# A hybrid attention and retention block on one core: the output projection from seven products of quarters

## The chip, the core and the metric

The kernel runs on one core of a Trainium2 chip. A core has TensorE (PE, matrix products), VectorE (DVE, elementwise work), ScalarE (ACT, elementwise functions and casts), GpSimd (POOL) and SyncE (SP, whose queue starts most transfers), each with a queue of its own that it works off in order. The metric is the device time of one execution in microseconds (us), the median of several runs. A profiled execution of the same program gives the trace, whose times count from the start of its span.

## The reference

512 tokens of 1024 channels, in float32. Two branches run side by side on the normalised tokens and are merged by sigmoid gates, one per channel; the merged rows go through the output projection and are added to the input:

```
p_a = jnp.einsum('bsw,wd->bsd', out_a, w_branch_sb[layer])
p_b = jnp.einsum('bsw,wd->bsd', out_b, w_branch_ret[layer])
merged = (jax.nn.sigmoid(m_sb + b_merge[layer, 0]) * p_a
          + jax.nn.sigmoid(m_ret + b_merge[layer, 1]) * p_b)
x = x + jnp.einsum('bsd,de->bse', merged, w_out[layer])
```

`out_a` is stick-breaking attention with 8 heads, gated; `out_b` is chunkwise retention with 4 heads, normalised and gated. All of their inputs are ten projections of the tokens by `w_in` (1024 x 10240).

## The kernel before

Every large product has 512 rows or columns in each operand and runs in `dense` (L211): four PSUM banks of 128x512, eight steps k over the contraction of 1024, and for each bank and step three matmuls (`mm3`, L91). There are three because both operands are kept as a pair of rounded numbers, a high part and a low part (`split`, L114: ScalarE casts the high part, VectorE subtracts it from the source for the low part), and the products high x high, high x low and low x high are added up. A `dense` call so has 4 x 8 x 3 = 96 matmuls of 512 columns. Weights come from `load_split` (L191): SP loads two steps at once (512 KB, two buffers `raw`), ScalarE and VectorE split them into `whi` and `wlo` (two buffers each), and the yield hands them to TensorE. These instructions have high priority: the scheduler, which sets the order of each queue, puts them ahead of others that it could place there. Matmuls and SP's loads keep the order of the program (`keep_in_program_order`).

Attention, retention and the like are generators that `work.step()` (an `Interleaver`, L40) advances between the matmuls of the projections. The order of the projections is the order of the calls from L523 on. The end of the program is: the retention's projections; the two gates `mb0`, `mb1`; `pb0` and `pb1` (two column groups g of `out_b` times its branch weights, banks transposed, so that a bank holds 128 channels of all tokens); behind each the merge (L573 to L577), four times a product with the gate, a sum with `pa[g]` and a split into `mg_hi` and `mg_lo`; then `fin0` and `fin1` (L581), the output projection's two halves of the columns, 192 matmuls together, whose banks hold 128 tokens and 512 output channels. VectorE adds each bank to the residual's tile `xr[g, tb]`, and a transfer stores it. In `fin1` the last two steps run bank by bank (`late`, L217), so that the banks end one after the other.

Of the kernel before, what the change touches and what calls it, by code (L numbers as in the profile page):

```python
# [33 lines left out]
V_BUFS = 14  # L34
# [33 lines left out]
def hybrid_block(ctx, tc, x, x_t, vecs, w_in, w_a, w_b, w_o, cos_t, sin_t, decay, out):  # L68
# [98 lines left out]
    idle = const.tile([P, S], mybir.dt.bfloat16, name="idle")  # L167
# [100 lines left out]
    def token_norm_rows():  # L268
# [5 lines left out]
        for tb in range(NT):  # L274
            rc = tmp.tile([P, P], F32, tag="rc", bufs=2, name="rc")
# [9 lines left out]
    def qk_group(p):  # L285
# [8 lines left out]
        for tb in range(NT):  # L294
            sq = tmp.tile([P, 4, P], F32, tag="sq", bufs=1, name="sqq")
# [34 lines left out]
    def v_group(name, c0):  # L330

        ps = proj(name, ((c0, S),), True)
        got = []
        for sb in range(NT):
            hi = big.tile([P, S], F32R, tag="V", bufs=V_BUFS, name=f"{name}_hi{sb}")
            lo = big.tile([P, S], F32R, tag="V", bufs=V_BUFS, name=f"{name}_lo{sb}")
            r = rx[:, sb : sb + 1]
            nc.scalar.activation(hi, ps[sb], AF.Copy, scale=r)
            nc.vector.scalar_tensor_tensor(lo, ps[sb], r, f32(hi), op0=ALU.mult, op1=ALU.subtract)
            got.append((hi, lo))  # L340
        return got
# [87 lines left out]
    def rope_group(h):  # L429
# [4 lines left out]
        ps[2:] = [big.tile([P, S], F32, tag="O", bufs=16, name=f"rk{h}_{j}") for j in range(2)]  # L434
# [17 lines left out]
    def retention(h, qk, v, gates):  # L452
        hi, lo = qk
        dec = tmp.tile([P, S], F32, tag="dec", bufs=1, name=f"dec{h}")
# [81 lines left out]
    rv[0] = v_group("rv0", C_RV)  # L536
# [113 lines left out]
```

## Time and profile before

| | us |
|---|---|
| median of 3 runs | 664.4 (664.32 to 664.45) |
| the profiled execution | 664.18 |
| its span | 662.4 |
| TensorE busy | 656.3 (99%) |
| VectorE busy | 375.9 (57%) |
| ScalarE busy | 260.7 (39%) |
| GpSimd busy | 50.8 (8%) |

Matmuls are pipelined: one lasts 0.39 us from start to end, and the next starts 0.23 us after it. So the busy share says that TensorE always had one in flight, and the spacing of the starts is what a matmul costs. A group's idle time and its releaser say what an engine waited for; idle time of an engine that nobody waits for costs nothing.

### The profile page before, as it was taken

The numbers are of one execution on the slowest core, as the hardware profiler recorded it, in microseconds if no ns is written. First come the engines' busy times: TensorE is split into PE (matmuls) and PEld (weight loads), VectorE is DVE, ScalarE is ACT, GpSimd is POOL, SyncE is SP. The second block draws the span as 40 slices with busy tenths as digits, with TensorE's granted clock in tenths as the row PEclk, the third lists the DMA queues.
The fourth block names the chain that finished last, engine by engine and source line by source line (L and its number), as shares of the span: only waits on it lengthen the run. The fifth ranks groups of instructions, "written<-read, shape, count | busy, mean of one in ns | idle before, by whom it ended". The sixth has DMA issues, their size and how long they took to land.

```text
span 662.4 us, 7979 instructions
## 1 busy us (share of the span) xinstructions
PE 656.3 (99%) x3096; PEld 546.4 (82%) x3096; DVE 375.9 (57%) x560; ACT 260.7 (39%) x416; POOL 50.8 (8%) x50
## 2 busy tenths in 40 slices
PE   8999999999999999999999999999999999999997
PEld 5888888888888888888888888888888888888886
DVE  6456874587497477632334763844862953544632
ACT  4744534464364554422312342433433443422310
POOL 0051000441000400000000001001001001000000
PEclk9999999999999999999999999999999999999999
DMA  8543223322322323233333323222323322335541
GB/s 288 189 128 96 65 63 96 96 64 65 95 64 64 96 63 96 60 99 96 95 96 111 96 64 106 84 80 81 96 70 106 93 66 64 96 95 161 158 159 63
DMA packets 42182, 65.02 MB, mean 98 GB/s; under 512 B 2848, under 2 KB 19488, under 8 KB 42144
## 3 DMA queue, kind: packets, MB, share of 16 engines
q1 hardware_dynamic: 41568, 63.47, 31.2%
q10 hardware_dynamic: 576, 1.05, 0.4%
q8 instruction: 24, 0.39, 0.3%
q14 instruction: 14, 0.11, 0.1%
HBM read 62.41 MB, written 2.10 MB: 97 GB/s over the span
## 4 chain that ended last, share of the span: by engine, by line
PE 99%; DMA 0%; SPq 0%; ACT 0%; DVE 0%; issue 0%; DVEq 0%; ACTq 0%
PE qk_ps L86 14%; PE rqk_ps L86 13%; PE sg_ps L86 7%; PE v_ps L86 7%; PE ma_ps L86 7%; PE rv_ps L86 7%; PE mb_ps L86 7%; PE rg_ps L86 7%; PE fin_ps L86 7%; PE pb_ps L86 7%; PE pa_ps L86 7%; PE po L86 2%; PE z L86 2%; PE rz L86 2%; PE ro L86 2%; PE pw L89 1%
## 5 line engine op out<-in xcount | busy, mean ns | idle before, releaser
L86 PE MATMUL qk_ps<-qk_hi,xT_hi 128*128 128x512 f32 x128 | 51.5, 411 | 0.9 <-ACT xT_hi L159 0.9
L86 PE MATMUL rqk_ps<-xT_hi,rqk_hi 128*128 128x512 f32 x128 | 50.5, 394 | 0.0
L86 PE MATMUL rqk_ps<-xT_hi,rqk_lo 128*128 128x512 f32 x128 | 50.0, 391 | 0.0
L86 PE MATMUL rqk_ps<-xT_lo,rqk_hi 128*128 128x512 f32 x128 | 50.0, 390 | 0.0
L86 PE MATMUL qk_ps<-qk_lo,xT_hi 128*128 128x512 f32 x128 | 49.8, 398 | 0.0
L86 PE MATMUL qk_ps<-qk_hi,xT_lo 128*128 128x512 f32 x128 | 49.5, 395 | 0.0
L86 PE MATMUL pb_ps<-ob,pb_hi 128*128 128x512 f32 x128 | 39.5, 390 | 0.0
L86 PE MATMUL pa_ps<-oa,pa_hi 128*128 128x512 f32 x128 | 39.4, 389 | 0.0
L116 DVE TENSOR_TENSOR rqk_lo<-rqk_raw,rqk_hi 128x1024 fp32r<-128x1024 f32 x16 | 20.8, 1300 | 23.9 <-ACT rqk_hi L115 23.9
L386 DVE TENSOR_TENSOR_SCAN keep<-keep,zero 128x128 f32<-128x128 f32 (+3 forms) x32 | 27.1, 847 | 7.3 <-ACT keep L384 7.3
L86 PEld LDWEIGHTS qk_ps<-qk_hi,xT_hi 128*128 128x128 f32 x128 | 24.5, 192 | 6.2 <-ACT xT_hi L159 1.8
L86 PEld LDWEIGHTS qk_ps<-qk_hi,xT_lo 128*128 128x128 f32 x128 | 24.5, 191 | 5.4
L189 POOL TENSOR_TENSOR rrr<-ms,m_half 128x4 f32<-128x4 f32 x4 | 4.0, 1007 | 316.3 <-DVE ms L188 316.3
L86 PEld LDWEIGHTS qk_ps<-qk_lo,xT_hi 128*128 128x128 f32 x128 | 24.7, 193 | 4.3
L86 PEld LDWEIGHTS rqk_ps<-xT_hi,rqk_lo 128*128 128x128 f32 x128 | 24.1, 188 | 5.0
L86 PEld LDWEIGHTS pb_ps<-ob,pb_hi 128*128 128x128 f32 x128 | 24.0, 188 | 5.0
L86 PEld LDWEIGHTS pa_ps<-oa,pa_hi 128*128 128x128 f32 x128 | 24.0, 188 | 5.0
L86 PEld LDWEIGHTS rqk_ps<-xT_hi,rqk_hi 128*128 128x128 f32 x128 | 24.1, 188 | 4.7
L86 PEld LDWEIGHTS rqk_ps<-xT_lo,rqk_hi 128*128 128x128 f32 x128 | 24.1, 188 | 4.6
L115 ACT CAST rqk_hi<-rqk_raw 128x1024 fp32r<-128x1024 f32 x16 | 16.8, 1050 | 25.8 <-PE rqk_ps L86 16.5
L116 DVE TENSOR_TENSOR qk_lo<-qk_raw,qk_hi 128x1024 fp32r<-128x1024 f32 x14 | 17.6, 1259 | 15.1 <-ACT qk_hi L115 15.1
L86 PE MATMUL v_ps<-v_hi,xT_hi 128*128 128x512 f32 x64 | 26.1, 408 | 0.0
(185 smaller groups left out, 1709.8 us busy)
## 6 DMA issues: line engine op xcount, KB each, us to landing
rqk_raw<-in_w_in SPq DMA_DIRECT2D x32, 256.0 KB, 3.0
qk_raw<-in_w_in SPq DMA_DIRECT2D x28, 256.0 KB, 3.0
v_raw<-in_w_in SPq DMA_DIRECT2D x8, 512.0 KB, 3.9
sg_raw<-in_w_in SPq DMA_DIRECT2D x8, 512.0 KB, 3.6
rv_raw<-in_w_in SPq DMA_DIRECT2D x8, 512.0 KB, 3.6
ma_raw<-in_w_in SPq DMA_DIRECT2D x8, 512.0 KB, 3.6
pa_raw<-in_w_a SPq DMA_DIRECT2D x8, 512.0 KB, 3.9
rg_raw<-in_w_in SPq DMA_DIRECT2D x8, 512.0 KB, 3.6
```

Of the source, the lines that this page charges most:

```text
L86: tc.keep_in_program_order(nc.tensor.matmul(*a, **k))
L89: tc.keep_in_program_order(nc.tensor.transpose(*a))
L115: nc.scalar.copy(hi, src)
L116: nc.vector.tensor_sub(lo, src, f32(hi))
L189: nc.gpsimd.tensor_tensor(dst, t[:, :width], m_half[:, :width], op=ALU.pow)
L386: nc.vector.tensor_tensor_scan(keep[:, :n][:, ::-1], keep[:, :n][:, ::-1], zero.broadcast_to([P, n]), 1.0, op0=ALU.mult, op1=ALU.add,)
```

## The change

The merged rows and `w_out` are cut into quarters: x11 is the first 256 tokens with the first 512 channels, x12 the same tokens with the other channels, x21 and x22 the other tokens; B11 to B22 are the quarters of `w_out` (512 x 512). The product of two such matrices needs eight products of quarters; here it is put together from seven, of sums of quarters. `strassen` runs them in the order 1, 2, 5, 3, 6, 7, 4:

- product 1 is x11 B11, product 2 is x12 B21, product 5 is s1 (B11 + B12) with s1 = x21 - x22, product 3 is n4 B22 with s2 = s1 - x11 and n4 = x12 + s2, product 6 is s2 (B11 + B12 + B22), product 7 is s3 (B12 + B22) with s3 = x11 - x21, product 4 is x22 (B21 + B11 + B12 + B22). The numbers are those of the code; the fourth in order is product 3, that of n4.
- a product is 2 halves of the contraction x 2 banks x 2 steps x 3 = 24 matmuls of 512 columns.
- the sums of the weights stand in four tiles X, Y, W, Z, in the place of v's: VectorE adds Y and later Z to X, and four transfers that GpSimd starts add to what is in Y and W. Each half of a piece is split into a high and a low part when its product comes near.
- the merged rows are kept in `pa` (whole numbers) and are split into `xT_hi` and `xT_lo`, where the tokens were. VectorE makes s1, s2 and n4 from `pa`, GpSimd makes s3, and each is split too.
- the products 1, 6, 7 and 4 add up in the same two banks `y`; after each product `put` adds its banks to residual tiles or subtracts them, and four of the seven also store.
- `late` now holds for `pb1`.
- the residual's second four loads come earlier, temporary tiles of equal size are shared (`bk` for beta, keep and the decay, `tmp` for the squares), v's rows are in whole tiles, the room for the descriptors of GpSimd's transfers is doubled, and `rv0` first drains the side work until head 3 is done.

```diff
--- before.py
+++ after.py
...
+    def O_tile(name):
+        return big.tile([P, 2, S], F32R, tag="O", bufs=8, name=name)
     def O_pair(name):
-        return [big.tile([P, S], F32R, tag="O", bufs=16, name=f"{name}_{q}") for q in range(2)]
+        t = O_tile(name)
+        return [t[:, q, :] for q in range(2)]
...
+    def V_tile(name, dtype=F32R):
+        return big.tile([P, 4, S], dtype, tag="V", bufs=4, name=name)
+    def bk_tile(name, dtype=F32):
+        return tmp.tile([P, 2, S], dtype, tag="bk", bufs=3, name=name)
...
-            if name == "fin1" and k >= NK - 2:
+            if name == "pb1" and k >= NK - 2:
...
+    def quarter(w, q):
+        return w[q].rearrange("p (k c) -> p k c", k=4)
+    def add_from(dst, src):
+        nc.gpsimd.dma_start(dst, src, accum_op=ALU.add)
+    def halves(t):
+        return t[:, :, :H], t[:, :, H:]
...
+    def made_sums(name, t):
+        hi, lo = (O_tile(f"{name}_{q}").rearrange("p a (b t) -> p (a b) t", b=2) for q in ("hi", "lo"))
+        split(hi, lo, t)
+        sums[name] = (hi, lo)
+    def quarter_sums(name, w, room):
+        n = [0]
+        def pair():
+            n[0] += 1
+            if n[0] % 3 == 1:
+                return bk_tile(f"{name}_bhi{n[0]}", F32R), bk_tile(f"{name}_blo{n[0]}", F32R)
+            return [
+                wpool.tile([P, 2, S], F32R, tag=f"w{q}", name=f"{name}_{q}{n[0]}") for q in ("hi", "lo")
+            ]
+        def part(t, h):
+            return t[:, 2 * h : 2 * h + 2, :]
+        def made(src):
+            hi, lo = pair()
+            split(hi, lo, src)
+            return hi, lo
+        X, Y, W, Z = room
+        with tc.high_priority():
+            for h in range(2):
+                load(part(X, h), part(quarter(w, B11), h))
+                load(part(Y, h), part(quarter(w, B12), h))
+            load(W, quarter(w, B21))
+            load(Z, quarter(w, B22))
+        for h in range(2):
+            with tc.high_priority():
+                got = made(part(X, h))
+                nc.vector.tensor_add(part(X, h), part(X, h), part(Y, h))
+                add_from(part(Y, h), part(quarter(w, B22), h))
+            yield got
+        for h in range(2):
+            with tc.high_priority():
+                got = made(part(W, h))
+            yield got
+        for h in range(2):
+            with tc.high_priority():
+                got = made(part(X, h))
+                nc.vector.tensor_add(part(X, h), part(X, h), part(Z, h))
+                add_from(part(W, h), part(X, h))
+            yield got
+        for t in (Z, X, Y, W):
+            for h in range(2):
+                with tc.high_priority():
+                    got = made(part(t, h))
+                yield got
+    def product(ps, left, pieces, first):
+        for h in range(2):
+            hi, lo = next(pieces)
+            for j in range(2):
+                js = slice(j * P, (j + 1) * P)
+                for i in range(2):
+                    k = 2 * h + i
+                    a, b = (t[:, k, js] for t in left), (hi[:, i, :], lo[:, i, :])
+                    ahi, alo = a
+                    for n, (u, v) in enumerate(((ahi, b[0]), (ahi, b[1]), (alo, b[0]))):
+                        matmul(
+                            ps[j], u, v, start=first and k == n == 0, stop=k == 3 and n == 2,
+                            skip_group_check=True,
+                        )
+                work.step()
+    def strassen(name, w, room, put):
+        def banks(n):
+            return [ps_mm.tile([P, S], F32, tag="mm", name=f"{name}_{n}{j}") for j in range(2)]
+        pieces = quarter_sums(name, w, room)
+        y = banks("y")
+        for n, a in ((1, "x11"), (2, "x12"), (5, "s1"), (3, "n4"), (6, "s2"), (7, "s3"), (4, "x22")):
+            ps = y if n in (1, 6, 7, 4) else banks(f"p{n}")
+            product(ps, tokens(a), pieces, n in (1, 2, 3, 5))
+            put(n, ps)
+    def tokens(a):
+        if a in sums:
+            return sums[a]
+        i, j = int(a[1]) - 1, int(a[2]) - 1
+        return [t[:, 4 * j : 4 * j + 4, i * H : (i + 1) * H] for t in (xT_hi, xT_lo)]
...
-    rv[0] = v_group("rv0", C_RV)
+    rv[0] = v_group("rv0", C_RV, lambda: 3 in oa)
...
     def residual(g):
-        yield 13
+        yield 13 if g == 0 else 1
...
-        hi, lo = T_tile(f"mg_hi{g}"), T_tile(f"mg_lo{g}")
         for j in range(4):
-            t = tmp_tile(f"mg{g}_{j}")
-            nc.vector.tensor_mul(t, ps[j], m[j])
-            nc.vector.tensor_add(t, t, pa[g][:, j, :])
-            split(hi[:, j, :], lo[:, j, :], t)
-        mt.append((hi, lo))
+            t, k = pa[g][:, j, :], 4 * g + j
+            nc.vector.tensor_mul(m[j], ps[j], m[j])
+            nc.vector.tensor_add(t, m[j], t)
+            split(xT_hi[:, k, :], xT_lo[:, k, :], t)
...
-        ps = dense(f"fin{g}", lambda k: tuple(t[:, k % 4, :] for t in mt[k // 4]), w_o, ((S * g, S),), True)
-        queue = nc.scalar if g == 0 else nc.sync
-        for tb in range(NT):
-            n = S // 2 if g == 1 and tb == NT - 1 else S
-            for c in range(0, S, n):
-                cs = slice(c, c + n)
-                nc.vector.tensor_add(xr[g, tb][:, cs], ps[tb][:, cs], xr[g, tb][:, cs])
-                queue.dma_start(out[tb * P : (tb + 1) * P, g * S + c : g * S + c + n], xr[g, tb][:, cs])
+    (x11, x21), (x12, x22) = halves(pa[0]), halves(pa[1])
+    nc.vector.tensor_sub(x22, x21, x22)
+    made_sums("s1", x22)
+    nc.vector.tensor_sub(x22, x22, x11)
+    made_sums("s2", x22)
+    nc.vector.tensor_add(x12, x12, x22)
+    made_sums("n4", x12)
+    nc.gpsimd.tensor_sub(x21, x11, x21)
+    made_sums("s3", x21)
+    def put(n, ps):
+        for j in range(2):
+            last = n == 4 and j == 1
+            g, tb, op = {
+                1: (0, j, ALU.add), 2: (0, j, ALU.add), 5: (1, 2 + j, ALU.add), 3: (1, j, ALU.add),
+                6: (1, j, ALU.subtract), 7: (1, 2 + j, ALU.subtract), 4: (0, 2 + j, ALU.add),
+            }[n]
+            with tc.high_priority():
+                for c in range(0, S, S // 2 if last else S):
+                    cs = slice(c, c + (S // 2 if last else S))
+                    t = xr[g, tb][:, cs]
+                    nc.vector.tensor_tensor(t, t, ps[j][:, cs], op=op)
+                    if n in (2, 6, 7, 4):
+                        queue = nc.scalar if n == 2 else nc.sync
+                        queue.dma_start(out[tb * P : (tb + 1) * P, g * S + cs.start : g * S + cs.stop], t)
+                if n == 5:
+                    t = xr[1, j]
+                    nc.vector.tensor_add(t, t, ps[j])
+    strassen("fin", w_oq, [V_tile(f"fin_w{n}", F32) for n in range(4)], put)
...
```

**Where the order changes.** VectorE's queue, from the second piece of the projection's weights on (in both it is the first row; `pb_ps` are the banks of `pb1`, `mb` its gates, `pa_2836` the second half of the merged rows, `fin_w` the weight tiles). Before:

```order
L116 TENSOR_TENSOR fin_lo_5022<-fin_raw_5019,fin_hi_5021 128x1024
L575 TENSOR_TENSOR mg_0_4995<-pb_ps_4861,mb_0_4703 128x512
L575 TENSOR_TENSOR mg_1_5000<-pb_ps_4862,mb_1_4706 128x512
L576 TENSOR_TENSOR mg_0_4995<-mg_0_4995,pa_2894 128x512
L576 TENSOR_TENSOR mg_1_5000<-mg_1_5000,pa_2894 128x512
L575 TENSOR_TENSOR mg_2_5005<-pb_ps_4863,mb_2_4709 128x512
L116 TENSOR_TENSOR fin_lo_5052<-fin_raw_5049,fin_hi_5051 128x1024
L576 TENSOR_TENSOR mg_2_5005<-mg_2_5005,pa_2894 128x512
L575 TENSOR_TENSOR mg_3_5010<-pb_ps_4864,mb_3_4712 128x512
L576 TENSOR_TENSOR mg_3_5010<-mg_3_5010,pa_2894 128x512
L116 TENSOR_TENSOR mg_lo_4994<-mg_0_4995,mg_hi_4993 128x512
L116 TENSOR_TENSOR mg_lo_4994<-mg_1_5000,mg_hi_4993 128x512
```

After:

```order
L129 TENSOR_TENSOR fin_lo_4982<-fin_w_4943,fin_hi_4981 128x1024
L690 TENSOR_TENSOR mb_0_4631<-pb_ps_4783,mb_0_4631 128x512
L404 TENSOR_TENSOR fin_w_4943<-fin_w_4943,fin_w_4944 128x1024
L691 TENSOR_TENSOR pa_2836<-mb_0_4631,pa_2836 128x512
L690 TENSOR_TENSOR mb_1_4634<-pb_ps_4784,mb_1_4634 128x512
L690 TENSOR_TENSOR mb_2_4637<-pb_ps_4785,mb_2_4637 128x512
L129 TENSOR_TENSOR xT_lo<-pa_2836,xT_hi 128x512
L129 TENSOR_TENSOR fin_lo_5012<-fin_w_4945,fin_hi_5011 128x1024
L691 TENSOR_TENSOR pa_2836<-mb_1_4634,pa_2836 128x512
L129 TENSOR_TENSOR fin_blo_5028<-fin_w_4945,fin_bhi_5027 128x1024
L691 TENSOR_TENSOR pa_2836<-mb_2_4637,pa_2836 128x512
L717 TENSOR_TENSOR xr_0_4973<-xr_0_4973,fin_y_4947 128x512
```

Before, the whole merge of the second half stands in a row with one split between. Now sums and splits of weights stand between its steps, and the merge of the last bank (`pb_ps_4786`) comes after these rows, behind two additions to the residual.

VectorE's queue further on (`s_lo` and `n_lo` are the low parts of s1 to s3 and of n4, `fin_p` the banks of the products 2, 5 and 3). Before, from the end of the merge:

```order
L116 TENSOR_TENSOR mg_lo_4994<-mg_3_5010,mg_hi_4993 128x512
L116 TENSOR_TENSOR fin_lo_5082<-fin_raw_5079,fin_hi_5081 128x1024
L116 TENSOR_TENSOR fin_lo_5112<-fin_raw_5109,fin_hi_5111 128x1024
L116 TENSOR_TENSOR fin_lo_5162<-fin_raw_5159,fin_hi_5161 128x1024
L588 TENSOR_TENSOR xr_0_4973<-fin_ps_5015,xr_0_4973 128x512
L588 TENSOR_TENSOR xr_1_4975<-fin_ps_5016,xr_1_4975 128x512
```

After, from the additions of product 2 on:

```order
L717 TENSOR_TENSOR xr_1_4975<-xr_1_4975,fin_p_5010 128x512
L129 TENSOR_TENSOR fin_blo_5092<-fin_w_4946,fin_bhi_5091 128x1024
L699 TENSOR_TENSOR pa_2836<-pa_2836,pa_2571 128x4x256
L701 TENSOR_TENSOR pa_2836<-pa_2836 128x4x256
L717 TENSOR_TENSOR xr_2_4997<-xr_2_4997,fin_p_5047 128x512
L129 TENSOR_TENSOR fin_lo_5108<-fin_w_4946,fin_hi_5107 128x1024
L717 TENSOR_TENSOR xr_3_4999<-xr_3_4999,fin_p_5048 128x512
L723 TENSOR_TENSOR xr_0_4993<-xr_0_4993,fin_p_5047 128x512
L723 TENSOR_TENSOR xr_1_4995<-xr_1_4995,fin_p_5048 128x512
L129 TENSOR_TENSOR fin_lo_5126<-fin_w_4943,fin_hi_5125 128x1024
L129 TENSOR_TENSOR s_lo<-pa_2836,s_hi 128x1024
L129 TENSOR_TENSOR n_lo<-pa_2836,n_hi 128x1024
```

Before, only splits of weights and the additions of a finished half are left. Now the sums of the rows and their splits stand between additions and splits of weights, and of these splits only that of s3 comes after `n_lo`.

ScalarE's queue around the projection's first matmul (`fin_w_4943` is X, `fin_w_4945` is W, `fin_w_4946` is Z). Before:

```order
L115 CAST pb_hi_4957<-pb_raw_4955 128x1024
L115 CAST fin_hi_5021<-fin_raw_5019 128x1024
L115 CAST fin_hi_5051<-fin_raw_5049 128x1024
L115 CAST mg_hi_4993<-mg_0_4995 128x512
L115 CAST mg_hi_4993<-mg_1_5000 128x512
```

After:

```order
L128 CAST fin_bhi_4955<-fin_w_4943 128x1024
L128 CAST pb_hi_4879<-pb_raw_4877 128x1024
L128 CAST fin_bhi_5027<-fin_w_4945 128x1024
L128 CAST fin_hi_4981<-fin_w_4943 128x1024
L128 CAST xT_hi<-pa_2836 128x512
```

The cast of the first piece of W (B21) now stands ahead of the cast of X's second half and of the merge's casts.

## Rows read from the trace of the kernel before

**Rows 1.** The page: span, part 1 (engine busy), part 4 (the last chain).
```profile
span 662.4 us, 7979 instructions
...
PE 656.3 (99%) x3096; PEld 546.4 (82%) x3096; DVE 375.9 (57%) x560; ACT 260.7 (39%) x416; POOL 50.8 (8%) x50
...
PE 99%; DMA 0%; SPq 0%; ACT 0%; DVE 0%; issue 0%; DVEq 0%; ACTq 0%
```

**Rows 2.** View of waits, TensorE: who was waited for, total, times, longest.
```profile
PE pi L86 <- DVE idle L168: 1.2, 1, 1.2
PE qk_ps L86 <- ACT xT_hi L159: 0.9, 1, 0.9
```

**Rows 3.** Timeline, TensorE: first and last projection matmul (start, duration us).
```profile
614.77 0.39 PE L86 MATMUL fin_ps<-fin_hi,mg_hi 128*128 128x512 f32 x1
...
658.06 0.39 PE L86 MATMUL fin_ps<-fin_hi,mg_lo 128*128 128x512 f32 x1
```

**Rows 4.** View by windows: length, busy time per engine, clock, DMA share, GB/s.
```profile
610.00:640.00 30.00, 30.00 (x134) 24.87 (x133) 17.47 (x22) 7.90 (x10) 0.00 (x0) 1.00 0.49 157
```

**Rows 5.** Timeline, ScalarE, before the projection's first matmul.
```profile
609.30 1.05 ACT L115 CAST fin_hi<-fin_raw 128x1024 fp32r<-128x1024 f32 x1 [4.34 <-PE pb_ps L86]
```

**Rows 6.** Timeline, VectorE, around the projection's first matmul.
```profile
610.38 1.23 DVE L116 TENSOR_TENSOR fin_lo<-fin_raw,fin_hi 128x1024 fp32r<-128x1024 f32 x1 [4.17 <-ACT fin_hi L115]
...
616.02 1.22 DVE L116 TENSOR_TENSOR fin_lo<-fin_raw,fin_hi 128x1024 fp32r<-128x1024 f32 x1
617.15 0.68 DVE L576 TENSOR_TENSOR mg<-mg,pa 128x512 f32<-128x512 f32 x1
617.75 0.68 DVE L575 TENSOR_TENSOR mg<-pb_ps,mb 128x512 f32<-128x512 f32 x1
```

**Rows 7.** Timeline, GpSimd, at 559 us.
```profile
558.98 2.04 POOL L495 TENSOR_TENSOR roraw<-roraw,rrr 128x512 f32<-128x512 f32 x2
```

**Rows 8.** Timeline, VectorE, the same microseconds.
```profile
560.49 1.61 DVE L116 TENSOR_TENSOR mb_lo<-mb_raw,mb_hi 128x1024 fp32r<-128x1024 f32 x1 [2.67 <-ACT mb_hi L115]
```

**Rows 9.** Timeline, VectorE, the last instructions.
```profile
658.48 0.76 DVE L588 TENSOR_TENSOR xr<-fin_ps,xr 128x256 f32<-128x256 f32 x2 [0.67 <-PE fin_ps L86]
```

**Rows 10.** Timeline, SyncE's queue: pb1's last load is the first row's third.
```profile
584.44 11.43 SPq L119 DMA_DIRECT2D pb_raw<-in_w_b  x3
595.92 2.32 SPq L119 DMA_DIRECT2D xr<-in_x  x4
```

**Rows 11.** View by windows: GB/s at the start and when the residual loads.
```profile
2.00:4.00 2.00, 2.00 (x6) 0.76 (x5) 0.42 (x1) 0.22 (x2) 0.00 (x0) 1.00 0.87 272
6.00:8.00 2.00, 2.00 (x6) 1.52 (x6) 1.41 (x3) 0.72 (x1) 0.00 (x0) 1.00 0.81 278
18.00:20.00 2.00, 2.00 (x10) 1.69 (x9) 0.03 (x1) 1.05 (x1) 0.00 (x0) 1.00 1.00 401
...
596.00:598.00 2.00, 2.00 (x11) 1.65 (x10) 1.91 (x5) 0.62 (x1) 0.00 (x0) 1.00 0.57 168
600.00:602.00 2.00, 2.00 (x10) 1.65 (x9) 1.38 (x2) 0.04 (x1) 0.00 (x0) 1.00 0.98 356
```

**Rows 12.** Timeline, TensorE, from the start of the program.
```profile
1.18 3.60 PE L86 MATMUL pi<-idle 128*128 128x512 bf16 x8 [1.18 <-DVE idle L168]
5.65 2.08 PE L86 MATMUL qk_ps<-qk_hi,xT_hi 128*128 128x512 f32 x4 [0.87 <-ACT xT_hi L159]
7.52 1.91 PE L86 MATMUL qk_ps<-qk_lo,xT_hi 128*128 128x512 f32 x4
9.23 1.46 PE L86 MATMUL qk_ps<-qk_hi,xT_lo 128*128 128x512 f32 x4
10.52 1.07 PE L86 MATMUL qk_ps<-qk_hi,xT_hi 128*128 128x512 f32 x4
```

More of the change, by code (lines that the diff above doesn't have):

```diff
@@ L26 @@
 C_MA, C_MB = 8192, 9216
+B11, B12, B21, B22 = range(4)
+H = S // 2
 V_NG, V_BM, V_QG, V_KG, V_RG, V_N = 0, 8, 24, 25, 26, 34
@@ L33 @@
 RAW_BUFS = 2
-V_BUFS = 14
 N_IDLE = 8
@@ L67, in hybrid_block @@
 @with_exitstack
-def hybrid_block(ctx, tc, x, x_t, vecs, w_in, w_a, w_b, w_o, cos_t, sin_t, decay, out):
+def hybrid_block(ctx, tc, x, x_t, vecs, w_in, w_a, w_b, w_oq, cos_t, sin_t, decay, out):
     nc = tc.nc
@@ L165, in hybrid_block @@
     first = first_loads()
-    idle = const.tile([P, S], mybir.dt.bfloat16, name="idle")
+    idle = tmp.tile([P, 2 * S], mybir.dt.bfloat16, tag="tmp", name="idle")[:, :S]
     nc.vector.memset(idle, 0.0)
@@ L259, in token_norm @@
                 s2 = small.tile([P, 2], F32, tag="s2", name="s2")
-                sq = tmp.tile([P, S], F32, tag="sq", bufs=1, name="sqx")
+                sq = tmp_tile("sqx")
                 for c in range(2):
@@ L274, in token_norm_rows @@
         for tb in range(NT):
-            rc = tmp.tile([P, P], F32, tag="rc", bufs=2, name="rc")
+            rc = tmp_tile("rc")[:, :P]
             nc.vector.tensor_copy(rc, rx[:, tb : tb + 1].broadcast_to([P, P]))
@@ L294, in qk_group @@
         for tb in range(NT):
-            sq = tmp.tile([P, 4, P], F32, tag="sq", bufs=1, name="sqq")
+            sq = tmp_tile("sqq").rearrange("p (h d) -> p h d", h=4)
             nc.scalar.activation(sq, raws[tb], AF.Square)
@@ L328, in qk_group, with v_group @@
             work.add(token_norm_rows())
-    def v_group(name, c0):
+    def v_group(name, c0, ready=lambda: True):
         ps = proj(name, ((c0, S),), True)
-        got = []
+        work.drain(ready)
+        hi, lo = V_tile(f"{name}_hi"), V_tile(f"{name}_lo")
         for sb in range(NT):
[L335 to L341, printed above, removed]
+            v_rows(hi, lo, sb, ps[sb])
+        return [(hi[:, sb, :], lo[:, sb, :]) for sb in range(NT)]
@@ L433, in rope_group @@
         hi, lo = T_tile(f"rqk_hi{h}"), T_tile(f"rqk_lo{h}")
-        ps[2:] = [big.tile([P, S], F32, tag="O", bufs=16, name=f"rk{h}_{j}") for j in range(2)]
+        ps[2:] = [tmp.tile([P, S], F32, tag="qraw", bufs=4, name=f"rk{h}_{j}") for j in range(2)]
         for j in range(2):
@@ L453, in retention @@
         hi, lo = qk
-        dec = tmp.tile([P, S], F32, tag="dec", bufs=1, name=f"dec{h}")
+        dec = bk_tile(f"dec{h}")[:, 0, :]
         load(dec, decay[h])
@@ L628, with quarters @@
     )
+    def quarters(w):
+        return np.stack(
+            [
+                w[i : i + S, j : j + S].reshape(4, P, S).transpose(1, 0, 2).reshape(P, 4 * S)
+                for i in (0, S)
+                for j in (0, S)
+            ]
+        )
     cos, sin, dec = _tables()
@@ L636 @@
         "w_b": np.asarray(w_branch_ret).reshape(D, D),
-        "w_o": np.asarray(w_out).reshape(D, D),
+        "w_oq": quarters(np.asarray(w_out).reshape(D, D)),
         "cos": cos,
```

17 lines of the change are left out of this document (10 added, 7 removed).

## The prediction

> **What bounds the kernel now.** I read the page first: TensorE is busy 99% of the span, and the chain of work that ended last is TensorE to 99%, with every other engine at 0% [rows 1]. The view of waits then says whether it ever stops: twice, 2.1 us in all, both in the first six microseconds [rows 2]. So the time is the number of matmuls times their spacing, and a removed matmul is worth its whole spacing as long as its operands still come in time. The stage of the change is the last one. Its first matmul starts at 614.77 us and its last, the 192nd, at 658.06 [rows 3], so the spacing is 43.29 / 191 = 0.2266 us. Call 614.77 T; all times below are counted from T. Ahead of T the change leaves the order of all 2900 matmuls as it is.
>
> The second thing to read is what feeds TensorE there. In the window 610 to 640 VectorE is busy 17.47 of 30 us and ScalarE 7.90 [rows 4]. That is the share that hides today, and it is what the change spends.
>
> **What goes away.** 7 products of 24 matmuls, all with 512 columns, are 168 in place of 192: 24 x 0.2266 = 5.44 us less TensorE work.
>
> **What is added on VectorE, and why it is on the path.** The queue of an engine is worked off in its order, so I count what stands in VectorE's queue ahead of the operands that TensorE wants. The start is anchored: a split of a piece of weights needs a buffer that TensorE frees 24 matmuls before T (T - 5.44), ScalarE casts, VectorE subtracts. Before, this cast is at 609.30 = T - 5.47 [rows 5] and the subtraction at 610.38 = T - 4.39 [rows 6]. The same pair of buffers stands in the same place after the change, so VectorE again starts at T - 4.39.
>
> From that instruction to the low part of the rows of the fourth product in order, that of n4 (n_lo, the last thing that this product waits for), the queue now holds 37 instructions. 17 have 1024 elements a lane: 8 splits of weight pieces, 3 sums of weight quarters, 3 sums of row quarters, 3 splits of such sums. 20 have 512: the merge of the four banks (4 products, 4 sums, 4 splits) and 8 additions of finished products into the residual. Start to start, 1024 elements take 617.15 - 616.02 = 1.13 us and 512 take 617.75 - 617.15 = 0.60 us [rows 6]. The sum is 17 x 1.13 + 20 x 0.60 = 31.2 us.
>
> Three hold-ups come on top. The split of the first sum (s1_lo) waits for ScalarE's cast of it, 1.05 us by the cast of the same size [rows 5], and only one addition (0.60) stands between: 0.5. VectorE reads results that it has only just written in four places; no row shows the price alone, so 0 to 1 us, and I take 0.5. The third is the subtraction on GpSimd for s3. It needs the same sum as s1, so it starts together with that cast; 1024 elements take 2.04 us as two halves [rows 7]. A VectorE subtraction with both inputs in SBUF that started at 560.49, while GpSimd ran until 561.02, took 1.61 us [rows 8], that is 0.53 of standing still and 1.08 of work. s1_lo falls inside GpSimd's 2.04 us and is held about 1.0 (0 if GpSimd is late, 2.0 if it comes just ahead). The Trainium skill says the same of the cause (SBUF — State Buffer, two separate sides): the two engines share a port pair that is an exclusive lock, and a VectorE operation with two SBUF inputs is blocked for the whole of a GpSimd instruction that reads SBUF. By that rule the hold-up is there and the sum is as it stands; with no lock it would be 1.0 less. The trace agrees with the rule, with the 1.61 us above.
>
> So n_lo ends at -4.39 + 31.2 + 0.5 + 0.5 + 1.0, and 0.1 until the result is written: T + 28.9. TensorE without any wait would ask for it at its 75th matmul, T + 74 x 0.2266 = T + 16.8. It waits 12.1 us up to there. Where these microseconds fall does not change the sum: about 3.5 us when the second half of product 2 wants the last merged bank (its multiplication stands behind two weight splits and the additions of product 1), 2 to 3 us for s1, 5 to 6 us for n4.
>
> From n_lo on 94 matmuls are left. VectorE is ahead again, but the running banks of products 1, 6, 7 and 4 are read by an addition before the next of these products adds to them. Between 1 and 6 other products run; 7 follows 6 and 4 follows 7 at once, and there TensorE waits for the addition: 0 to 0.7 each (one addition), I take 0.4, together 0.8. After the last matmul nothing changes: the last bank is still added in two halves [rows 9], and it still ends six matmuls after the one before it.
>
> **What is added on the queues.** SP now issues six loads of weights, 4.19 MB, at once behind pb1's last load, and the residual's eight loads stand behind them. That last load goes out at about 595.5 and the residual's follow at 595.92 [rows 10], so the weights start there. ScalarE's cast of the first piece of B21 stands ahead of the cast that anchors VectorE, and it waits for a 1 MB load that is the fifth in line: 3.67 MB with pb1's load. By an estimate bytes flow from 596.9 on (168 GB/s over 596 to 598), and with the queue full they flow at 272 to 401 GB/s [rows 11]. B21 lands between 606.1 and 610.4; it is wanted at 609.30 - 1.05 = 608.25. So it costs 0 to 2.1 us; at 360 GB/s it is 607.1 and costs nothing. But GpSimd's first adding transfer (0.52 MB) runs in the same time and would take 1.4 us of that rate: 608.5. I take 0.3. The residual's last load waits for the merge of the last bank at some T + 8 and is used at T + 22, which hides it. The other adding transfers (no row shows one) are issued by T + 13 and wanted at T + 34 and T + 39; up to 20 us each is hidden. The two stores on ScalarE's queue wait for product 2's additions, and the casts of s2 and n4 stand behind them; these end some 4 us before n_lo, so VectorE stays last.
>
> **The other edits** (shared temporary tiles, values in whole tiles, the drain ahead of rv0): taken at 0. TensorE's order is the same and it waits nowhere there [rows 2], so they cannot gain; VectorE at 57% and ScalarE at 39% [rows 1] cover them. If a shared tile is held too long, it shows as a wait of the size of the two in [rows 2], so 0 to 1.2 us.
>
> **The sum.** -5.44 + 12.1 + 0.8 + 0.3 = +7.8 us. The profiled execution took 664.18 us, its span 662.4 and 1.8 around it; the median of the runs is 664.4, 0.2 above. 664.18 + 7.8 = 672.0, and 672.2 for a median.
>
> **Rivals.**
> *VectorE is not the bound and the saved matmuls are the whole story.* TensorE's 99% and VectorE's 17.47 of 30 us speak for it. It decides at n_lo: at T + 16.8 or sooner the time is 664.4 - 5.4 = 659.0; up to T + 21.4 (16.8 + 5.44 - 0.8) it is not slower than before. For that VectorE must do the 37 instructions in 19.1 to 23.7 us in place of 31.2 (2.0 us more if nothing holds it up), or start 7.5 us sooner than its buffer allows. No row shows a two-input operation of 512 elements under 0.60.
>
> *The clock falls in the pauses.* At the start, with TensorE fresh from idling and again after a pause of 0.87 us, four matmuls take 7.52 - 5.65 = 1.87 us, 0.47 each, and it is not before 10.52 that four take 0.91, 0.227 each [rows 12], though the granted clock reads 1.00 throughout [rows 11]. 512 columns in 0.42 to 0.47 us is the 1.2 GHz level. The trace of before holds no later pause. After it there are pauses of some 3.5 us and of 2 and 3.4 us nearly end to end. Price: the second half of product 2 (12 matmuls) takes 12 x 0.2 = 2.4 us more, and an addition that VectorE's queue waits for passes on about 2; after the last pause 4 us at half rate, as from 5.65, lose 2, and 8 us, as from 1.18, lose 4. Together +4 to +6: 676 to 678. The Trainium skill (TensorE: Matmul & The Clock Gate, why this matters for your kernels) asks for no long pauses between bursts of matmuls, since the clock then goes back to half; by that rule this rival is the forecast. The trace agrees only in that a start from idle is slow.
>
> *The weights come late.* Adding transfers cost the queue more than their bytes, and B21 lands 4 to 6 us after 608.25; each microsecond moves the whole of VectorE's stretch: 676 to 678. The low rate of 272 GB/s speaks for it, the 401 against it.
>
> **Chances.** Forecast 0.66 (from +4.7, with no hold-up, late wait or late load, to +11.7, with all at their upper ends: 669.1 to 676.1), clock 0.19, weights 0.08, VectorE not the bound 0.05, a mixture that lands within 0.2%, which is about what a measurement can tell from no change, 0.02. The range 668.5 to 678 takes in the first three. Faster by over 0.2% 0.05, within it 0.02, slower 0.93.
>
> **What would show it.** Right: in the profile after, TensorE has 24 matmuls fewer and some 13 us of waits, all after the first projection matmul, on VectorE and ScalarE; VectorE is busy nearly without a gap from T - 4 to T + 29 while TensorE is not; the longest waits are at the last merged bank and at n4; the tail after the last matmul is the old 4.3 us. The lock shows as an s1_lo of about 2 us. Wrong: TensorE keeps its 99%; or the matmuls after the pauses are 0.4 us apart (clock); or ScalarE's cast of B21 ends later than T - 5.5 and waits for its load (weights); or waits turn up ahead of T (the other edits).

## The result, and the profile after

The changed kernel takes 673.3 us, the median of four runs (672.20 to 674.52), against 664.42 for the kernel before in the same job (664.32 to 664.57): a ratio of 1.0143, 95% interval 1.0128 to 1.0158. It is slower, and 673.3 lies 1.1 us above the predicted 672.2 and inside the range.

The page of the profiled execution (672.84 us) answers to [rows 1]: 24 matmuls fewer, VectorE 22.7 us busier, and the chain that ended last is no longer TensorE alone. The PEclk row, in tenths of full speed over 40 slices, has two slices below 9 near its end.

```profile
span 671.1 us, 7980 instructions
...
PE 654.5 (98%) x3072; PEld 542.2 (81%) x3072; DVE 398.6 (59%) x585; ACT 269.3 (40%) x426; POOL 53.6 (8%) x55
...
PEclk9999999999999999999999999999999999999879
...
PE 91%; DVE 5%; DMA 2%; issue 1%; ACT 1%; SPq 0%; DVEq 0%; ACTq 0%
```

The view of waits for TensorE (total us, times, longest) answers to [rows 2]. Everything new lies in the last stage, 10.6 us in all, on VectorE and ScalarE.

```profile
PE fin_p L89 <- ACT xT_hi L128: 3.6, 1, 3.6
PE fin_p L89 <- DVE n_lo L129: 2.9, 1, 2.9
PE fin_p L89 <- ACT n_hi L128: 2.1, 1, 2.1
PE pi L89 <- DVE idle L181: 1.2, 1, 1.2
PE qk_ps L89 <- ACT xT_hi L172: 1.0, 1, 1.0
PE fin_p L89 <- DVE s_lo L129: 1.0, 1, 1.0
PE fin_y L89 <- DVE xr L717: 0.7, 2, 0.4
PE fin_p L89 <- DVE xT_lo L129: 0.4, 1, 0.4
```

The first and the last projection matmul, the timeline of TensorE, answer to [rows 3]. T is now 612.77, and the last matmul starts 54.09 us later, where it was 43.29.

```profile
612.77 0.39 PE L89 MATMUL fin_y<-fin_bhi,xT_hi 128*128 128x512 f32 x1
...
666.86 0.39 PE L89 MATMUL fin_y<-fin_hi,xT_lo 128*128 128x512 f32 x1
```

So the stage is 10.80 us longer, and yet the span only 8.7: T itself is 2.00 us earlier than in [rows 3]. That gain is the start of the program. In [rows 12] three groups of four matmuls are slow; here none is, the groups start 0.9 to 1.0 apart from 5.75 on:

```profile
5.75 1.19 PE L89 MATMUL qk_ps<-qk_hi,xT_hi 128*128 128x512 f32 x4 [0.96 <-ACT xT_hi L172]
6.78 1.08 PE L89 MATMUL qk_ps<-qk_lo,xT_hi 128*128 128x512 f32 x4
7.69 1.07 PE L89 MATMUL qk_ps<-qk_hi,xT_lo 128*128 128x512 f32 x4
```

The view by windows of the last stage (length, busy time with counts for PE, PEld, DVE, ACT, POOL, then granted clock, DMA share, GB/s) shows the rest. The first of these rows is the stretch that the prediction's queue of 37 instructions fills: VectorE is busy 32.86 of its 33.45 us. The other rows are two short stretches behind TensorE's long pauses and one behind its short one.

```profile
608.80:642.25 33.45, 23.53 (x93) 17.76 (x91) 32.86 (x38) 13.52 (x15) 5.01 (x4) 0.91 0.54 132
...
626.40:629.60 3.20, 3.17 (x8) 2.49 (x9) 2.67 (x3) 1.04 (x1) 2.42 (x2) 0.50 1.02 205
632.00:636.00 4.00, 4.00 (x19) 3.29 (x18) 3.96 (x5) 2.00 (x2) 0.00 (x0) 1.00 0.18 66
...
642.30:646.70 4.40, 4.40 (x10) 3.51 (x11) 1.23 (x2) 0.00 (x0) 0.00 (x0) 0.50 0.00 0
```

TensorE's granted clock is 0.50, its 1.2 GHz level, from 626.4 on, behind the pause that ended at 625.34, and behind the two that ended at 638.65 and 642.30; behind the wait of 1.0 us for s1 it is 1.00. The matmuls show it by their spacing, 0.43 us:

```profile
638.65 0.51 PE L89 MATMUL fin_p<-fin_bhi,n_hi 128*128 128x512 f32 x1 [2.14 <-ACT n_hi L128]
...
642.30 0.80 PE L89 MATMUL fin_p<-fin_bhi,n_lo 128*128 128x512 f32 x1 [2.92 <-DVE n_lo L129]
642.89 0.63 PE L89 MATMUL fin_p<-fin_bhi,n_hi 128*128 128x512 f32 x1
643.32 0.63 PE L89 MATMUL fin_p<-fin_blo,n_hi 128*128 128x512 f32 x1
...
646.73 0.40 PE L89 MATMUL fin_p<-fin_hi,n_hi 128*128 128x512 f32 x1
646.96 0.40 PE L89 MATMUL fin_p<-fin_lo,n_hi 128*128 128x512 f32 x1
```

From 642.30 to 646.73 ten matmuls start, in 4.43 us where 10 x 0.2266 = 2.27 would do: 2.2 us lost. The timelines of ScalarE, VectorE and GpSimd show the queue's start and the lock:

```profile
606.77 1.05 ACT L128 CAST fin_bhi<-fin_w 128x1024 fp32r<-128x1024 f32 x1 [3.82 <-DMA fin_w<-in_w_oq]
607.73 1.04 ACT L128 CAST fin_hi<-fin_w 128x1024 fp32r<-128x1024 f32 x1
```

```profile
608.80 1.23 DVE L129 TENSOR_TENSOR fin_lo<-fin_w,fin_hi 128x1024 fp32r<-128x1024 f32 x1 [4.02 <-ACT fin_hi L128]
...
628.75 2.43 DVE L129 TENSOR_TENSOR s_lo<-pa,s_hi 128x1024 fp32r<-128x1024 f32 x1 [0.52 <-ACT s_hi L128]
631.11 0.67 DVE L717 TENSOR_TENSOR xr<-xr,fin_p 128x512 f32<-128x512 f32 x1
...
641.03 1.22 DVE L129 TENSOR_TENSOR n_lo<-pa,n_hi 128x1024 fp32r<-128x1024 f32 x1
```

```profile
627.72 2.37 POOL L703 TENSOR_TENSOR pa<-pa 128x1024 f32<-128x1024 f32 x1 [0.78 <-DVE pa L697]
```

### The profile page after: what moved, and what is told of

Its sections match the earlier page's. It is cut to its first block, busy times and chain, and to the rows that moved or that the text cites. A ratio compares the mean times of both kernels' runs of the same rounds, so it can differ in the third digit from the quotient of the medians.

```text
span 671.1 us, 7980 instructions
## 1 busy us (share of the span) xinstructions
PE 654.5 (98%) x3072; PEld 542.2 (81%) x3072; DVE 398.6 (59%) x585; ACT 269.3 (40%) x426; POOL 53.6 (8%) x55
## 4 chain that ended last, share of the span: by engine, by line
PE 91%; DVE 5%; DMA 2%; issue 1%; ACT 1%; SPq 0%; DVEq 0%; ACTq 0%
PE qk_ps L89 13%; PE rqk_ps L89 13%; PE sg_ps L89 7%; PE v_ps L89 7%; PE ma_ps L89 7%; PE rv_ps L89 7%; PE mb_ps L89 7%; PE rg_ps L89 7%; PE pa_ps L89 6%; PE pb_ps L89 4%; PE po L89 2%; PE z L89 2%; PE rz L89 2%; PE ro L89 2%; PE fin_y L89 2%; DMA fin_w<-in_w_oq 2%
## 5 line engine op out<-in xcount | busy, mean ns | idle before, releaser
L503 DVE TENSOR_TENSOR_SCAN beta<-beta,zero 128x128 f32<-128x128 f32 (+3 forms) x32 | 26.9, 840 | 7.8 <-ACT beta L501 7.8
```

Of the source, the lines that this page charges most:

```text
L503: nc.vector.tensor_tensor_scan(keep[:, :n][:, ::-1], keep[:, :n][:, ::-1], zero.broadcast_to([P, n]), 1.0, op0=ALU.mult, op1=ALU.add,)
```

## The experiments

The times of one kernel vary by 2 us and more, before's too (662.34 to 664.40 in one job), so I compare the stage, from the first projection matmul's start to the last one's, in the profiled execution; the start of the program is not in it. Each stage below is that of a single execution, and stages vary as well: e4's runs lie 3.3 us apart, more than the start explains (T differs by 2.4 us among the ten profiled executions). So a difference of 1 us between two stages counts only where the rows show what it is made of. The extra matmuls of e2 and e5 do not count as waits.

| kernel | stage us | waits in it | median of runs |
|---|---|---|---|
| before | 43.29 | 0 | 664.42 |
| after | 54.09 | 10.6 | 673.3 |
| e1, two halves again | 43.29 | 0 | 662.62 (10 runs) |
| e2, pauses filled | 53.80 | 3.4 | 673.84 (4) |
| e3, s3 on VectorE | 53.09 | 9.2 | 673.52 (4) |
| e4, two products swapped | 47.75 | 5.7 | 668.45 (4) |
| e5, e4 with one pause filled | 48.95 | 4.7 | 669.11 (5) |
| e6, a written order | 39.20 | 0.3 | 658.15 (5) |
| e7, e6 with ten idle matmuls | 39.21 | 0.3 | 658.04 (4) |
| e8, eight additions later | 49.42 | 7.3 | 668.97 (4) |

**e1, the seven products undone.**

```diff
-    strassen("fin", w_oq, [V_tile(f"fin_w{n}", F32) for n in range(4)], put)
+    for g in range(2):
+        ps = dense(f"fin{g}", lambda k: (xT_hi[:, k, :], xT_lo[:, k, :]), w_o, ((S * g, S),), True)
...
```

> The seven products are undone: the last projection is again two halves of 96 matmuls in before's order, while all the other edits stay (merged rows in the tokens' place, shared temporary tiles, values in whole tiles, the drain ahead of rv0). The trace of after reaches its first projection matmul 2.0 us earlier than that of before, because the matmuls of the first stage run 0.227 us apart from 5.75 us on in place of 0.47. Theory A: this comes with the other edits, which otherwise cost and gain nothing: 664.4 - 2.0 = 662.4 us, no wait of TensorE ahead of the last stage, last stage 43.3 us from first to last matmul. Theory B: it comes with the execution and not with the edits: 664.4, and the start is slow or quick as it falls. Theory C: the other edits cost something at the end (rows merged in place): above 664.9, with waits on VectorE or ScalarE in the last stage.

662.62 us (662.02 to 664.22) against 664.03 for before (662.34 to 664.40), ratio 0.9987, interval 0.9976 to 0.9998. The first and the last projection matmul:

```profile
614.33 0.39 PE L89 MATMUL fin_ps<-fin_hi,xT_hi 128*128 128x512 f32 x1
...
657.62 0.39 PE L89 MATMUL fin_ps<-fin_hi,xT_lo 128*128 128x512 f32 x1
```

The stage is the old one to the hundredth and nothing waits ahead of it, so theory C is out: the other edits cost nothing. The start was slow in the profiled execution (T = 614.33), though the edits are all in it, and both kernels' runs cover the same 2 us: theory B, the start falls by the execution. The traces agree: their first clock record begins at 10.02 us in before's execution, 9.58 in e1's and 5.00 in after's, and there the matmuls turn quick. The median 1.4 us lower says at most that it falls quick more often here; why is open. All of the loss belongs to the seven products.

**e2, the pauses filled.** An extra matmul multiplies merged rows that are long ready into a bank that nobody reads.

```diff
+                        if (n0, h, j, i, n) in FILL:
+                            fill(FILL[n0, h, j, i, n])
...
+    FILL = {(2, 1, 0, 1, 0): 15, (5, 0, 0, 0, 2): 4, (3, 0, 0, 0, 0): 9, (3, 0, 0, 0, 2): 12}
```

> After, with 40 extra matmuls of 512 columns that fill most of the four pauses: 15 ahead of the matmul that waited 3.6 us, 4 ahead of the one that waited 1.0, 9 and 12 ahead of those that waited 2.1 and 2.9 (15 x 0.227 = 3.4, 0.9, 2.0, 2.7 us). They multiply rows that are long ready, into a bank that nobody reads. Clock theory: TensorE does not stop, so no stretch of matmuls 0.43 us apart is left; the end comes 2.0 us sooner (the stretch behind n_lo lies on the path, the one behind the last merged bank does not): 672.8 - 2.0 = 670.8, and the runs spread less. Rival: the matmuls behind a pause are slow for another reason (their operands, the weight loads, VectorE's traffic): the 0.43 us spacing stays in the same places, and the time is 672.8 or more, since the fillers are in the way.

The view by windows: behind the filled pause in product 2, behind a pause of 0.5 and 2.0 us that stayed at s1, and behind the filled ones at n4.

```profile
627.40:629.70 2.30, 1.87 (x7) 1.22 (x7) 2.19 (x3) 1.07 (x2) 1.52 (x2) 1.00 1.00 201
633.80:636.50 2.70, 2.70 (x8) 2.13 (x7) 2.67 (x3) 1.05 (x1) 0.00 (x0) 0.50 0.00 0
645.30:648.00 2.70, 2.70 (x13) 2.25 (x12) 0.85 (x2) 0.24 (x1) 0.00 (x0) 1.00 0.00 0
```

Where TensorE did not stop for more than 0.5 us, the clock stays at 1.00 with the same operands; where it still stopped for 2.0, it falls. That is the clock theory, and the rival is out. The 2 us were gained where they were expected, but lost again ahead of that place. The rows are n_lo on VectorE, its first matmul and the last matmul (T = 613.83):

```profile
643.33 1.22 DVE L129 TENSOR_TENSOR n_lo<-pa,n_hi 128x1024 fp32r<-128x1024 f32 x1
```

```profile
645.29 0.39 PE L89 MATMUL fin_p<-fin_bhi,n_lo 128*128 128x512 f32 x1
...
667.63 0.39 PE L89 MATMUL fin_y<-fin_hi,xT_lo 128*128 128x512 f32 x1
```

From that matmul to the last one it takes 22.34 us, where after takes 24.56: 2.2 less. But the matmul itself starts at T + 31.46, where after's starts at T + 29.53. Of these 1.9 us, 1.2 are n_lo's result, which comes at T + 30.72 in place of T + 29.48: the scheduler moved two of VectorE's instructions ahead of s1's low part, the pause at s1 grew, nine matmuls behind it lost 1.7 us at half rate, and VectorE then stood 1.71 us for a cast of weights that waited for TensorE. The other 0.7 are the extra matmuls, still running when n_lo was there. So the stage is 0.3 shorter and not 2.0, the median is 673.84 in place of 670.8, and the runs lie 3.0 us apart (671.14 to 674.12), not closer.

**e3, the lock.**

```diff
-    nc.gpsimd.tensor_sub(x21, x11, x21)
+    with tc.issue_after(done["n4"].ins):
+        nc.vector.tensor_sub(x21, x11, x21)
```

> After, with the subtraction for s3 on VectorE right behind the low part of n4 in place of GpSimd; everything ahead of that keeps its place in VectorE's queue. Theory (lock on the path): the low part of s1 takes 1.22 us in place of 2.43, n_lo ends 1.2 us sooner, TensorE's waits on s1 and n4 shrink by 1.2 in sum, and the time is 671.6. Rival (the hold-up is absorbed, since TensorE waits for ScalarE's casts as well): s1's low part is quicker, but n_lo and the end come within 0.3 us of where they were. The runs of after lie 2.3 us apart, so the profile decides.

VectorE's timeline, s1's low part, the addition of product 2 behind it, and n_lo:

```profile
628.70 1.23 DVE L129 TENSOR_TENSOR s_lo<-pa,s_hi 128x1024 fp32r<-128x1024 f32 x1 [0.51 <-ACT s_hi L128]
629.84 0.68 DVE L718 TENSOR_TENSOR xr<-xr,fin_p 128x512 f32<-128x512 f32 x1
...
639.79 1.22 DVE L129 TENSOR_TENSOR n_lo<-pa,n_hi 128x1024 fp32r<-128x1024 f32 x1
```

1.23 us in place of 2.43, n_lo 1.24 earlier (T is 612.79), the wait for s1 gone from the view of waits, the stage 1.00 shorter (the stretch at half rate is one matmul longer). So the lock was on the path: 1.2 us of VectorE's queue, 1.0 of the stage. The runs (671.86 to 673.87) can't tell it from after's.

**e4, n4 asked for later.**

```diff
-        for t in (Z, X, Y, W):
+        for t in (X, Z, Y, W):
...
-        for n, a in ((1, "x11"), (2, "x12"), (5, "s1"), (3, "n4"), (6, "s2"), (7, "s3"), (4, "x22")):
+        for n, a in ((1, "x11"), (2, "x12"), (5, "s1"), (6, "s2"), (3, "n4"), (7, "s3"), (4, "x22")):
...
-                    if n in (2, 6, 7, 4):
+                    if n in (2, 3, 7, 4):
```

> After, with the product of s2 ahead of that of n4 (order 1, 2, 5, 6, 3, 7, 4; the weight pieces follow their products). n4's rows are then asked for 24 matmuls = 5.44 us later. VectorE's work is the same, except that the split of s2 moves ahead of the weight pieces of the later products. Theory (the time is set by when the products' operands leave VectorE's queue): the waits of 2.1 and 2.9 us for n4 go nearly whole and no new one of their size comes at s2, whose rows are ready by about 22.9 us after the first projection matmul, when TensorE, held up by the last merged bank and by s1 as before (some 8 us), wants them; the stage is some 4.5 us shorter and the slow stretch behind n_lo goes with its pause (2 us): 666.3, between 665.5 and 668.5. Rival (VectorE's total up to the end of its stretch decides, whatever the order): the wait reappears at s2 and at the weight pieces, and the time is 672 to 674.

668.45 us (666.42 to 669.75), ratio to before 1.0071, interval 1.0047 to 1.0095. The stage is 6.34 shorter, where 4.5 + 2 was expected. In the view of waits n4 costs 0.2 in place of 5.0 and s2 costs nothing:

```profile
PE fin_p L89 <- ACT xT_hi L128: 3.0, 1, 3.0
PE fin_p L89 <- DVE s_lo L129: 2.2, 1, 2.2
...
PE fin_p L89 <- DVE n_lo L129: 0.2, 1, 0.2
```

So not VectorE's total decides, but when TensorE asks for what. The scheduler changed one more thing: here the addition of product 2 and a split of weights stand ahead of s1's low part. The addition waits for TensorE, and the wait for s1 is 2.2 in place of 1.0:

```profile
629.57 0.69 DVE L717 TENSOR_TENSOR xr<-xr,fin_p 128x512 f32<-128x512 f32 x1 [1.59 <-PE fin_p L89]
```

**e5, e4 with the pause in product 2 filled.** The edit is e2's, with `FILL = {(2, 1, 0, 1, 0): 12}`.

> The kernel with the two products swapped, and 12 extra matmuls of 512 columns (2.7 us; rows that are long ready, into a bank that nobody reads) ahead of the matmul that waits 3.0 us for the last merged bank. VectorE's and ScalarE's queues stay as they are, in the same order. In the swapped kernel ten matmuls behind that pause are 0.43 us apart or more, and VectorE's addition of product 2 stands 1.59 us for TensorE. Clock theory: TensorE does not stop, the second half of product 2 runs 0.227 apart, VectorE's addition no longer waits, s1's low part and all that follows come 1.6 us sooner: stage (first to last projection matmul) 46.1 in place of 47.75. Rival (the matmuls are slow for another reason, or the slow stretch is absorbed): stage 47.5 to 48.

The stage is 1.2 longer, so the expectation fails, and the rows say how. Product 2's second half now runs at 1.00 and VectorE's addition doesn't wait for TensorE. But VectorE then meets GpSimd's subtraction of 2.38 us: the instruction ahead of s1's low part is held for 1.0, which in e4 fell into the wait for TensorE. s1 comes only 0.34 us sooner, TensorE is there more than 1 us sooner, waits 0.4 and 2.9 us for it, and runs at 0.50 behind that. The first row is VectorE's timeline, the second the view by windows:

```profile
630.54 2.23 DVE L129 TENSOR_TENSOR fin_blo<-fin_w,fin_bhi 128x1024 fp32r<-128x1024 f32 x1
```

```profile
634.30:637.00 2.70, 2.70 (x8) 2.11 (x7) 2.67 (x3) 1.05 (x1) 0.00 (x0) 0.50 0.00 0
```

Again the half rate goes with the pause and not with the operands. But a pause that is filled is not a wait that is gone: what VectorE has not done is asked for all the sooner. The medians, 669.11 and 668.45, are too close to tell this by themselves.

**e8, eight additions behind n4.** (Product 5's two banks come from the pool that is free by then.)

```diff
-            put(n, ps)
+            held.append((n, ps))
+            if n not in (1, 2, 5):
+                with tc.issue_after(done["n4"].ins):
+                    for m in held:
+                        put(*m)
```

> After, in the order of products that after has, with one thing moved: the eight additions of products 1, 2 and 5 into the residual (8 x 0.60 = 4.8 us of VectorE) stand behind the low part of n4 in place of ahead of it, and product 5 goes to two banks that are free by then. Theory (the wait for n4 is VectorE's queue, instruction by instruction): n4's rows are ready 3 to 4.8 us sooner, the stage is 3 to 4 us shorter (50 to 51 in place of 54.1), with a new short wait where a late addition frees a bank. Rival (the pauses only move to another place): 53 us or more.

n_lo on VectorE (T = 613.09), and the longest waits of the stage:

```profile
634.87 1.23 DVE L129 TENSOR_TENSOR n_lo<-pa,n_hi 128x1024 fp32r<-128x1024 f32 x1
```

```profile
PE fin L89 <- ACT s_hi L128: 4.7, 1, 4.7
...
PE fin L89 <- DVE s_lo L129: 1.3, 1, 1.3
```

The stage is 4.67 shorter, more than the 3 to 4 that were expected; but more was moved than the eight additions. The scheduler put two splits of weights behind n_lo as well, so VectorE's queue up to it has 27 instructions in place of 37, and n_lo's result comes at T + 23.01 in place of T + 29.48. The 6.5 us are 8 x 0.60 + 2 x 1.13 = 7.1, less 0.6 because s1's low part waits longer for ScalarE's cast (1.11 in place of 0.52). n4 is not waited for any more; s1's rows are, 4.7 and 1.3 us, a wait that takes in what the last merged bank's was. What the additions alone are worth is not shown.

**e6, the order written out.** The work is that of e3, in e4's order of products, with some weight pieces split in two halves of 512, and with product 5 and one bank of product 3 in the other pool of banks; each instruction of VectorE and ScalarE is pinned behind the one ahead of it in the text. Its core:

```diff
+RING = ("bk", "qraw", "tmp", "w", "w")
...
+    p3 = piece_hi(part(W, 1))
+    piece_lo(p2)
+    low(2)
+    low(3)
+    prod(1, "x11")
+    pin(nc.vector.tensor_sub(x22, x21, x22))
+    p4 = piece_hi(part(X, 0))
+    sum_hi("s1", x22)
+    piece_lo(p3)
+    prod(2, "x12")
+    piece_lo(p4)
+    p5 = piece_hi(part(X, 1))
+    sum_lo("s1", x22)
+    plus(X, Z, 0)
...
```

> The seven products with VectorE's and ScalarE's work of the last stage in a written order: the swapped order of products; merges of the last four banks first, each sum and its split as early as its product needs it; five pairs of buffers for weight pieces in place of three (the two more in tiles that lie idle by then); the additions of finished products 2 and 5 behind everything that a product waits for; the subtraction for s3 on VectorE. The sum of VectorE's work is the same but for GpSimd's subtraction (+1.1 us). Theory (what bounds after is the order in which VectorE reaches the operands, not their number): TensorE waits 0.5 to 2.5 us in all, no pause is long enough for a slow stretch, the stage is 168 x 0.2266 + 1 to 2.5 = 39 to 40.5 us in place of 54.09 and of before's 43.29: 658.0 to 661.0 us, below before. Rival (VectorE's total is too much for 38 us of TensorE in any order): waits of 5 us and more stay, 664 or above.

658.15 us (658.01 to 659.84), ratio to before 0.9913, interval 0.9899 to 0.9927: 5.7 us faster than before in the same job, and 15 us below after's median. Waits of TensorE, and a window from four microseconds ahead of its first projection matmul (614.65) to 32 behind it:

```profile
PE pi L90 <- DVE idle L182: 1.2, 1, 1.2
PE qk_ps L90 <- ACT xT_hi L173: 0.7, 1, 0.7
PE fin_y L90 <- DVE fin_lo L698: 0.3, 1, 0.3
```

```profile
610.68:646.65 35.97, 35.52 (x156) 28.69 (x155) 35.80 (x46) 17.50 (x23) 2.64 (x3) 1.00 0.43 108
```

VectorE is as full as in after, 35.80 of 35.97 us, and TensorE 35.52, at a granted clock of 1.00 throughout. 39.20 us is 167 x 0.2266 = 37.84 and 1.4. Stage and time lie in the ranges that were expected, and the rival is out.

**e7, e6 with ten idle matmuls at the start.** The edit is one number, `N_IDLE = 10` in place of 8.

> The kernel with the written order, and 10 in place of 8 idle matmuls at the start, which reach nearly up to the first matmul of the program (there is a pause of 0.5 to 1.3 us behind the eight). Theory (the 2.0 us by which executions of one kernel differ are the matmuls of the first stage, slow or quick by what TensorE did in that pause): the first matmuls are 0.23 apart in every execution, the runs lie within 0.5 us, at the lower end of the kernel with eight: 1 us or more below its median. Rival: the pause has nothing to do with it, the spread of 2 us stays, and the median is that of the kernel with eight, within 0.4.

658.04 us (657.55 to 658.58), ratio to before 0.9912, interval 0.9898 to 0.9926; not told from e6. The profiled execution started quick, but the ten took no longer than the eight (3.68 us against 3.59), so the pause stayed, 0.64 us. The experiment did not do what it was to do; it settles nothing about the start.

## Why the prediction was right, and where not

- *24 matmuls fewer, VectorE bounds the stage.* Right, and shown from both sides: with the products undone nothing waits (e1), and with nearly the same work reordered the waits go (e4, e6). So the bound is VectorE's queue in the order in which it stood, and not the sum of its work.
- *The queue of 37.* 33.3 us were predicted, from T - 4.39 to n_lo's result at T + 28.9; 33.45 were measured, from 608.80 = T - 3.97 to 642.25 = T + 29.48. The sum was right to a per cent, since each duration came from a row of the same size. Its three hold-ups were taken at 0.5, 0.5 and 1.0 and came to about 0.6, 0.3 and 1.2.
- *The lock.* Predicted 1.0 for s1's low part, measured 2.43 - 1.22 = 1.2, and by e3 on the path. GpSimd's 1024 elements took 2.37 us in one piece, where [rows 7] gave 2.04 for two halves. The Trainium skill's rule (SBUF — State Buffer, two separate sides) agrees with the 2.43, and with 1.23 once GpSimd is out.
- *B21.* Predicted 0.3, measured 0.43: its cast waited for the load until 606.77, so the next one, which anchors VectorE, starts at 607.73 = T - 5.04, where it was T - 5.47 [rows 5].
- *The bank waits.* 0.8 predicted. With the restart of the matmuls behind them they and the rest of the way cost 1.3: from 646.73 to 666.86 83 matmuls should take 18.81 us, and take 20.13.
- *The clock.* This is the step that failed: it was at nothing in the sum and among the rivals with 0.19, and it came. Behind n_lo it cost 2.2 us, near the lower of the two prices there (2). Its other half did not come: the half rate in product 2 was to be passed on by VectorE's addition, but that addition (631.11) waits for nothing, since s1's low part stands ahead of it in VectorE's queue. In e3, without the lock, it waits for nothing either (629.84); in e4, where it stands ahead of s1's low part, it waits 1.59. What product 2 lost at half rate, 1.6 us, TensorE would else have stood for s1: that wait is 1.0 where 2 to 3 were forecast, and the waits together are 10.6 where some 13 were. The Trainium skill's rule (TensorE: Matmul & The Clock Gate, why this matters for your kernels), no long pauses between bursts, agrees with the 0.50 behind the pause of 3.6 us and the two of 2.1 and 2.9; the wait of 1.0 was followed by 1.00. The prediction's reading that the clock is 1.00 at the start [rows 11] is none: the trace of before holds no clock record ahead of 10.02 us, and the view prints 1.00 where it has none.
- *The other edits at 0.* Right (e1).

The stage was forecast at 43.29 + 7.8 = 51.1 us and took 54.09: 0.3 of the 3.0 is n_lo's lateness, 2.2 the clock, 0.5 the bank waits. That the time still came within 1.1 us of the forecast is because the start of the profiled execution was 2.0 us quicker than that of before's. Started like [rows 12], this execution would have taken 674.8. So the direction and the bound were right by their reasons, and that the time came so close is luck: two misses cancel.

What the prediction did not see is that the loss was not in the idea. It counted VectorE's 37 instructions as a sum that has to be done; it did not ask which of them TensorE needs by then. The eight additions need not stand there (e8, with two splits of weights: 4.7 us of the stage), n4 need not be fourth (e4: 6.3), the subtraction on GpSimd need not run beside s1 (e3: 1.0). All of it together, with the merges first and five pairs of buffers for weight pieces, is 14.9 us (e6); what the buffers, the merges or the other banks give alone was not tried.

## What to carry to other kernels

An algebraic trick that trades matmuls for vector work is decided by the order in which the vector engine reaches the operands: list its queue with the moment at which TensorE asks for each result, before judging the sum. Here the kernel gave the additions of finished products high priority, and the scheduler put them ahead of operands; writing the order out, with two more pairs of buffers, took the stage from 54.1 to 39.2 us with nearly the same instructions. And price a pause of TensorE at more than its length, by what the matmuls behind it do, where no later wait takes that in.

## What the runs showed of the hardware

- Behind the pauses of 3.6 us and of 2.1 and 2.9 in a row (after) and of 0.5 and 2.0 (e2) the granted clock read 0.50 for 7, 10 and 9 matmuls, 1.6, 2.2 and 1.7 us lost. It read 0.50 as well behind 0.4 and 2.9 (e5), 3.0 (e4) and 4.7 and 1.3 (e8). Behind 1.0 us (after), and behind 2.2 us right after such a stretch (e4), the matmuls were quick.
- At the start of the program matmuls are 0.47 us apart, in before's execution up to some 10 us [rows 12]. The view by windows prints a clock of 1.00 there [rows 11], but the trace holds no record of the clock ahead of 10.02 us: the spacing tells it.
- That moment differs by execution: the first clock record of the ten profiled ones begins between 3.96 and 10.60 us, between none and twelve of the first matmuls were slow, and T lies between 612.34 and 614.77.
- A VectorE subtraction of 1024 elements with both inputs in SBUF took 2.43 us beside a GpSimd subtraction of 2.37 (after) and 1.23 without it (e3).
- An adding transfer of 0.52 MB held GpSimd for 0.9 to 1.1 us and landed 5.4 us (from SBUF) or 7.7 us (from DRAM) after its issue, as medians of two each; in after none was waited for on TensorE's path.
